# A two-layer decoder step on one core: layer 0's copies, its norm's bias and the opening's squares on other engines

## The chip, the cores and the metric

One core of one Trainium2 chip runs the whole program. The metric is the device time of one execution in microseconds. A core has five engines that matter here: TensorE (PE, matrix products, with a separate row PEld for its weight loads), VectorE (DVE), ScalarE (ACT), GpSimd (POOL), and SyncE (SP), whose queue issues all loads and stores of this kernel.

## The reference, cut to what matters

Two layers for 512 prompt positions and 32 sample positions (8 sequences of 4), model width 1024, all in fp32. Layer 0 norms its input, multiplies it by one wide matrix, and splits the columns into attention heads and convolution channels:

```
h = _rms(x, norm_g)
q, k, v, g_att, u_a, u_b, g_conv = _split(h @ w_in, AB_SPLITS)
q = _rms(q.reshape(B, T, ATT_HEADS, ATT_HEAD_DIM), q_g)
k = _rms(k.reshape(B, T, ATT_HEADS, ATT_HEAD_DIM), k_g)
u = u_a * jax.nn.sigmoid(u_b)
...
y = jax.nn.silu(_layernorm(y, ln_g, ln_b))
...
m = jnp.concatenate([o_att * jax.nn.silu(g_att), o_conv * jax.nn.silu(g_conv)], axis=-1)
return x + m @ w_out
```

`_rms` divides by the root of the mean square over the 1024 features and scales by `norm_g`. The prompt attends within blocks of 256 positions and to the earlier block; the samples attend to cached keys and values, which are gathered page by page. The convolution has 31 taps; its result goes through a layer norm with gain `ln_g` and bias `ln_b`. Layer 1 is a gated linear recurrence with its own projections; the change does not touch it.

## The kernel before, in words

**Layout.** Activations lie with features on the 128 partitions and the 544 positions along the row: `xT[k]`, k = 0..7, is 128 features by 544 positions. Every product is split in precision: a factor a is kept as a rounded high part and a low part a - high, and `unit` (L137) adds three passes for each k: high weight x high activation (L142), high weight x low activation (L143), low weight x high activation (L144). A unit makes 128 output features for one half (272) of the positions in one of three PSUM banks "g". `wtile` (L127) loads a weight tile from memory on SP's queue, makes its high part on ScalarE (L133) and its low part on VectorE (L134).

**Order.** The program is written with a tile framework (L1072) that plays it on its own model of the engines when it is built and chooses the order of each engine's instructions from that, on the queues of SP and GpSimd as well; at a few places an order is pinned by hand (`issue_after`). A changed engine for one instruction can therefore change the order of others.

**The opening** (L178 to L310) is written as steps "sA u nA u r sB w e a nB" (L292) on the two halves of the positions. `squares` (L256) makes the squares of the 8 feature tiles, two at a time (four instructions, the engine of each from `SQ` for the first half and `SQB` for the second: `sqg` on GpSimd at L186, `sqa` on ScalarE at L180, `sqv` on VectorE at L183), and for the first half also the gained inputs `xg` (L189 on ScalarE, L192 on VectorE). Three adds follow: squares 0 and 1 on GpSimd (L265), squares 2 and 3 on VectorE (L266), then both sums on VectorE (L267). `norms` (L249) sums over the partitions with PE (L252), takes the root on ScalarE (L253) and the reciprocal on VectorE (L254). Meanwhile two units "u" run in plain fp32 on `xg` (L230), `rawsplit` makes high (L272, ScalarE) and low (L273, VectorE) parts of the second half, `wsplits` the weight parts wh (L281) and wl (L282), and step "e" scales the two finished units by the norm (L235), which frees their PSUM banks. The third and fourth unit (L363, L142 to L144) need L273, L282, and a free bank.

**After the opening** three constants are cast to bf16 (`identb`, `causb`, `smb`, L312 to L317) for the masks of attention. For each of four pairs of heads `prepkq` (L388) projects and norms keys and queries: the keys are turned by PE, copied by ScalarE (L404), normed, stored, turned back, and copied out of PSUM (L447 on ScalarE; the sample columns `ksT` on VectorE, L448). `prepvg` (L451) projects the values, turns them, copies them out of PSUM (`vt` L462 and `vsn` L463, VectorE) and stores them. The turned tiles take two PSUM banks "t", which the attention's transposes share. `attend` (L478) does the attention of a pair; its exponentials are L496. The taps of the convolution (L379) run on VectorE all along.

**The layer norm** of the convolution (L555 to L595) ends, for each of 4 channel tiles and 2 halves, in a multiplication by gain and 1/deviation (L586, VectorE), the addition of the bias (L587, VectorE), a tanh (L589, ScalarE) and two products (L590, L591, VectorE). Beside it the cached key pages are loaded (L606) for the sample attention.

Of the kernel before, what the change touches and what calls it, by code (L numbers as in the profile page):

```python
# [13 lines left out]
AF = mybir.ActivationFunctionType  # L14
ALU = mybir.AluOpType
# [5 lines left out]
TS = 32  # L21
# [8 lines left out]
C_CAUS = 256  # L30
C_SM = 384
# [35 lines left out]
def hybrid_step(ctx, tc, xt_in, cache_kt, cache_v, conv_in, hgrn_in, page_table, par_in, k_norm_0,  # L67
# [3 lines left out]
    V, A, G, PE, SP = nc.vector, nc.scalar, nc.gpsimd, nc.tensor, nc.sync  # L71
# [17 lines left out]
    cst = cp.tile([128, C_END], F32, name="cst")  # L89
# [67 lines left out]
    def vec(name, k=0):  # L157
        return vecs[:, vidx[name] + k:vidx[name] + k + 1]
# [19 lines left out]
    with tc.tile_pool(name="l0", bufs=1) as lp:  # L178
# [13 lines left out]
            V.tensor_scalar(xg[k][:, hs], xT[k][:, hs], vec("n0", k), None, op0=ALU.mult)  # L192

        SQ = (sqg, sqa, sqa, sqv)
        SQB = (sqg, sqa, sqa, sqv)
        XG = (xga, xgv, xga, xgv, xga, xgv, xga, xgv, )
        NM = (V, V, V, V, V, V, V, V, )
        xg = [mtile(("xg", k), F32) for k in range(KT)]
# [57 lines left out]
        def squares(hf):  # L256
            sq = []
            for i in range(4):
                q = mk(lp, "kn", [128, T], 8).rearrange("p (a t) -> p a t", a=2)
                (SQ, SQB)[hf][i](q, xTall[:, 2 * i:2 * i + 2, HC[hf]])  # L260
                sq.append(q)
                if hf == 0:
                    for k in (2 * i, 2 * i + 1):
                        XG[k](k, HC[0])
            G.tensor_tensor(sq[0], sq[0], sq[1], op=ALU.add)  # L265
            V.tensor_tensor(sq[2], sq[2], sq[3], op=ALU.add)  # L266
            V.tensor_tensor(sq[0], sq[0], sq[2], op=ALU.add)  # L267
            return sq[0]
# [41 lines left out]
                norm_a()  # L310

        identb = lp.tile([128, 128], BF16, name="identb")  # L312
        G.tensor_copy(identb, ident)
        causb = lp.tile([128, 128], BF16, name="causb")
        G.tensor_copy(causb, cst[:, C_CAUS:C_CAUS + 128])
        smb = lp.tile([128, 64], BF16, name="smb")
        G.tensor_copy(smb, cst[:, C_SM:C_SM + 64])  # L317
        qbd = lp.tile([128, 4, NS, 32], F32, name="qbd")
        G.memset(qbd, 0.0)
        ksT = lp.tile([128, 4, TS], F32, name="ksT")  # L320
# [67 lines left out]
        def prepkq(c):  # L388
            col = c * 128
            kr = mk(lp, "kr", [128, T], 2)  # L390
            w = wtile(w_in_0, 512 + col)
            for hf in range(2):
                unit_to(kr, w, hf)
            kt = mk(lp, "kt", [128, 5, 128], 2)
            ksq = mk(lp, "P", [128, 512], 2).rearrange("p (i d) -> p i d", i=4)
            ksqs = mk(lp, "ksqs", [TS, 128], 1)
            ssk = mk(lp, "ssk", [128, 24], 2)
            pk = bank("t")
            pks = bank("t")
            for i, n, sl in TOK:  # L400
                transpose(pk[:, i * 128:(i + 1) * 128] if i < 4 else pks[:n, :128], kr[:, sl], 128)
            for pq, i0, i1, n, so in ((pk, 0, 4, 128, ksq), (pks, 4, 5, TS, ksqs.unsqueeze(1))):
                p3 = pq[:n, :(i1 - i0) * 128].rearrange("p (i d) -> p i d", d=128)
                A.activation(kt[:n, i0:i1], p3, AF.Copy)  # L404
                A.activation(so, p3, AF.Square)
            V.reduce_sum(ssk[:, 0:8], ksq.rearrange("p i (h d) -> p (i h) d", d=64), axis=AX.X)
            V.reduce_sum(ssk[:TS, 8:10], ksqs.rearrange("p (h d) -> p h d", d=64), axis=AX.X)

            w = wtile(w_in_0, col)
            qT = mk(lp, "qT", [128, T], 2)  # L410
            sq = mk(lp, "sq", [128, T], 1)
            for hf in range(2):
                unit_to(qT, w, hf)
                A.activation(sq[:, HC[hf]], qT[:, HC[hf]], AF.Square)
            pssq = bank("t")
            for i in range(4):
                PE.matmul(pssq[:, 2 * i:2 * i + 2], sq[:, i * 128:(i + 1) * 128], blk[:, 0:128:64], start=True, stop=True)
            PE.matmul(pssq[:, 8:8 + TS], blk, sq[:, TP:T], start=True, stop=True)
            rq = mk(lp, "rq", [128, 40], 2)
            rk = mk(lp, "rk", [128, 10], 2)  # L420
            A.activation(rq, pssq[:, 0:40], AF.Sqrt, bias=eps)
            A.activation(ssk[:, 0:8], ssk[:, 0:8], AF.Sqrt, scale=1.0 / 64, bias=eps)
            A.activation(ssk[:TS, 8:10], ssk[:TS, 8:10], AF.Sqrt, scale=1.0 / 64, bias=eps[:TS])
            V.reciprocal(rk[:, 0:8], ssk[:, 0:8])
            V.reciprocal(rk[:TS, 8:10], ssk[:TS, 8:10])
            V.reciprocal(rq, rq)
            for hh in range(2):
                r = slice(64 * hh, 64 * hh + 64)
                o = (2 * c + hh) * 4
                V.scalar_tensor_tensor(qbd[r, c, :, o:o + 4], qT[r, TP:T].rearrange("p (n t) -> p n t", t=4),  # L430
                                       gq8[r], rq[r, 8:40].rearrange("p (n t) -> p n t", t=4),
                                       op0=ALU.mult, op1=ALU.mult)
            kT = kz[c % 2]
            for i0, i1, n in ((0, 4, 128), (4, 5, TS)):
                k3 = kt[:n, i0:i1].rearrange("p i (h d) -> p (i h) d", d=64)
                nb = 2 * (i1 - i0)
                V.tensor_tensor(k3, k3, rk[:n, 2 * i0:2 * i1].unsqueeze(2).to_broadcast([n, nb, 64]), op=ALU.mult)
                V.tensor_tensor(k3, k3, gk_bc[:n].unsqueeze(1).to_broadcast([n, nb, 64]), op=ALU.mult)
            SP.dma_start(k_prompt[0].rearrange("(i p) h d -> p i (h d)", p=128)[:, :, col:col + 128], kt[:, 0:4])
            SP.dma_start(k_sample.rearrange("n t h d -> (n t) (h d)")[:, col:col + 128], kt[:TS, 4])  # L440
            pk = bank("t")
            pks = bank("t")
            for i, n, sl in TOK:
                transpose(pk[:, sl] if i < 4 else pks[:, :n], kt[:n, i], n)
            for hh in range(2):
                r = slice(64 * hh, 64 * hh + 64)
                A.activation(kT[r, hh], pk[r], AF.Copy, scale=gq8[r, 0:1])  # L447
            V.tensor_copy(ksT[:, c], pks[:, :TS])  # L448
            return c, rq, qT, kT

        def prepvg(c, rq, qT, kT):  # L451
            col = c * 128
            w = wtile(w_in_0, 1024 + col)
            vr = mk(lp, "kr", [128, T], 2)
            for hf in range(2):
                unit_to(vr, w, hf)
            vt = mk(lp, "vt", [128, 4, 128], 2)
            pk = bank("t")
            pks = bank("t")
            for i, n, sl in TOK:  # L460
                transpose(pk[:, i * 128:(i + 1) * 128] if i < 4 else pks[:n, :128], vr[:, sl], 128)
            V.tensor_copy(vt.rearrange("p i d -> p (i d)"), pk)  # L462
            V.tensor_copy(vsn[:, col:col + 128], pks[:TS, :128])  # L463
            SP.dma_start(v_prompt[0].rearrange("(i p) h d -> p i (h d)", p=128)[:, :, col:col + 128], vt)
            SP.dma_start(v_sample.rearrange("n t h d -> (n t) (h d)")[:, col:col + 128], vsn[:, col:col + 128])

            w = wtile(w_in_0, 1536 + col)
            ga = mk(lp, "ga", [128, T], 2)
            for hf in range(2):
                unit_to(ga, w, hf)  # L470
                tg = mk(lp, "tb", [128, HALF], 3)
                A.activation(tg, ga[:, HC[hf]], AF.Tanh, scale=0.5)
                V.scalar_tensor_tensor(ga[:, HC[hf]], tg, 1.0, ga[:, HC[hf]], op0=ALU.add, op1=ALU.mult)
            G.tensor_scalar(gas[:, c], ga[:, TP:T], 0.5, 0.0, op0=ALU.mult, op1=ALU.add)

            return c, rq, qT, kT, vt, ga
# [105 lines left out]
        for c in range(4):  # L582
            tgs = []
            for hf in range(2):
                hs = HC[hf]
                V.scalar_tensor_tensor(cy[c][:, hs], cy[c][:, hs], vec("lg", c), rss[hf], op0=ALU.mult, op1=ALU.mult)  # L586
                V.tensor_scalar(cy[c][:, hs], cy[c][:, hs], vec("lb", c), None, op0=ALU.add)  # L587
                tg = mk(lp, "ct", [128, HALF], 2)
                A.activation(tg, cy[c][:, hs], AF.Tanh, scale=0.5)  # L589
                V.scalar_tensor_tensor(tg, tg, 1.0, cy[c][:, hs], op0=ALU.add, op1=ALU.mult)  # L590
                V.scalar_tensor_tensor(tg, tg, 0.25, gc[c][:, hs], op0=ALU.mult, op1=ALU.mult)  # L591
                tgs.append(tg)
            mh, ml = mtile(("h", 4 + c)), mtile(("l", 4 + c))
            for hf in range(2):
                split(mh[:, HC[hf]], ml[:, HC[hf]], tgs[hf])  # L595
# [485 lines left out]
```

## Time and profile before

| | |
|---|---|
| median of 3 runs | 655.58 us (653.95 to 656.63) |
| the profiled execution | 655.62 us, of it span 652.9 us |
| PE busy in the span | 629.5 us, 5806 instructions |
| DVE busy | 524.8 us, 1252 instructions |
| ACT busy | 365.5 us, 908 instructions |
| POOL busy | 62.7 us, 91 instructions |

The profile is that of one execution. "Busy" is the time in which an engine has an instruction under way; matmuls are pipelined, so a busy PE need not be at its peak rate. The granted clock of TensorE (PEclk) is 1.00 at 2.4 GHz and 0.50 at 1.2 GHz. In a row of the timeline the bracket at the end gives the time for which the engine stood idle before the instruction, and the engine, tile and line that ended this wait.

### The profile page before, as it was taken

What the parts mean: (1) busy time and instruction counts of PE and PEld (TensorE: products, weight loads), DVE (VectorE), ACT (ScalarE), POOL (GpSimd) and SP (SyncE); (2) the same over time, 40 slices, a digit from 0 to 9 for tenths busy, and PEclk for the clock granted to TensorE, in tenths of its full rate; (3) what the DMA queues carried; (4) which work ended last, traced back from release to release, by engine and by line L of the source; (5) the groups of instructions that cost most, each with busy time, mean ns of one, the idle gap of its engine ahead of it and who ended that gap; (6) DMA issues with size and microseconds to landing.
All of it is one profiled execution on the core that took longest, in us unless ns stands there. A gap on an engine that the chain in (4) does not pass through costs nothing.

```text
span 652.9 us, 14858 instructions
## 1 busy us (share of the span) xinstructions
PE 629.5 (96%) x5806; PEld 581.9 (89%) x5806; DVE 524.8 (80%) x1252; ACT 365.5 (56%) x908; POOL 62.7 (10%) x91
## 2 busy tenths in 40 slices
PE   8799999999999986999989999999999999999997
PEld 6699998997996855879989999999999999999997
DVE  6999989889889857666978988878787878866656
ACT  7344486487378674445755664646464646447321
POOL 6100000000100000000011211111111110121000
PEclk9799999999999997999999999999999999999999
DMA  8434311221242047446442232323223232322114
GB/s 297 121 82 111 113 56 66 84 83 65 80 84 81 22 139 241 155 143 213 162 146 102 70 113 84 107 93 102 99 99 102 84 117 69 115 78 94 46 58 149
DMA packets 39015, 70.56 MB, mean 108 GB/s; under 512 B 11938, under 2 KB 20642, under 8 KB 38946
## 3 DMA queue, kind: packets, MB, share of 16 engines
q1 hardware_dynamic: 38946, 69.63, 33.6%
q8 instruction: 45, 0.74, 0.5%
q14 instruction: 24, 0.20, 0.1%
HBM read 59.88 MB, written 9.73 MB: 107 GB/s over the span
## 4 chain that ended last, share of the span: by engine, by line
PE 88%; DVE 4%; DMA 3%; ACT 3%; SPq 1%; issue 1%; DVEq 0%; ACTq 0%
PE g L142 23%; PE g L143 23%; PE g L144 22%; PE t L102 5%; PE s L484 2%; PE o L508 2%; DMA kn<-in_cache_kt_dram 2%; PE o L952 1%; PE t L939 1%; PE s L847 1%; DMA kn<-in_cache_v_dram 1%; PE s L612 1%; PE s L853 1%; DMA xTall<-in_xt_dram 1%; PE o L954 1%
## 5 line engine op out<-in xcount | busy, mean ns | idle before, releaser
L142 PE MATMUL g<-h,wh 128*128 128x272 f32 x944 | 278.9, 296 | 5.3 <-DVE ct L235 2.7
L143 PE MATMUL g<-h,wh 128*128 128x272 f32 x944 | 277.9, 295 | 1.9 <-DVE h L273 1.7
L144 PE MATMUL g<-h,wl 128*128 128x272 f32 x944 | 275.4, 292 | 0.0
L142 PEld LDWEIGHTS g<-h,wh 128*128 128x128 f32 x944 | 179.7, 190 | 9.7 <-ACT f L743 3.1
L143 PEld LDWEIGHTS g<-h,wh 128*128 128x128 f32 x944 | 179.6, 190 | 6.0 <-DVE h L273 3.1
L144 PEld LDWEIGHTS g<-h,wl 128*128 128x128 f32 x944 | 179.5, 190 | 1.7 <-issue 1.2
L133 ACT ACTIVATE wh<-wr 128x1024 fp32r<-128x1024 f32 (+4 forms) x90 | 88.1, 981 | 91.1 <-PE g L143 84.5
L134 DVE TENSOR_TENSOR wl<-wr,wh 128x1024 fp32r<-128x1024 f32 (+4 forms) x90 | 101.1, 1125 | 26.4 <-ACT wh L133 25.6
L379 DVE SCALAR_TENSOR_TENSOR m<-m,vecs,m 128x512 f32<-128x512 f32 x120 | 87.5, 741 | 0.7
L142 PE MATMUL g<-m,wh 128*128 128x272 f32 x256 | 74.0, 293 | 0.3 <-ACT wh L133 0.3
L144 PE MATMUL g<-m,wl 128*128 128x272 f32 x256 | 74.1, 291 | 0.0
L143 PE MATMUL g<-m,wh 128*128 128x272 f32 x240 | 69.6, 290 | 0.0
L142 PEld LDWEIGHTS g<-m,wh 128*128 128x128 f32 x256 | 47.9, 188 | 2.6 <-DVE m L106 0.8
L144 PEld LDWEIGHTS g<-m,wl 128*128 128x128 f32 x256 | 48.1, 189 | 1.0 <-issue 0.8
L143 PEld LDWEIGHTS g<-m,wh 128*128 128x128 f32 x240 | 45.2, 188 | 1.1 <-DVE ct L590 0.8
L959 ACT ACTIVATE S<-S,tot 128x128 f32<-128x128 f32 x64 | 20.5, 390 | 11.4 <-PE t L858 11.4
L484 PE MATMUL s<-kz,qT 128*128 128x128 f32 (+3 forms) x64 | 22.8, 447 | 1.4 <-ACT PP L496 1.3
L916 DVE TENSOR_TENSOR qq<-qq,tot 128x256 f32<-128x256 f32 x24 | 11.7, 486 | 14.8 <-PE s L888 12.0
L503 ACT ACTIVATE PT<-t 128x128 f32<-128x128 f32 (+3 forms) x32 | 13.9, 433 | 14.7 <-PE t L102 14.6
L961 POOL TENSOR_TENSOR ve<-vx,cst 128x1024 fp32r<-128x1024 f32 x8 | 16.1, 2019 | 49.8 <-DVE vx L736 30.0
L1020 DVE TENSOR_TENSOR xTall<-g,xTall 128x272 f32<-128x272 f32 x32 | 13.5, 437 | 8.8 <-PE g L144 8.3
L917 DVE TENSOR_TENSOR kk<-kk,tot 128x256 f32<-128x256 f32 (+1 forms) x48 | 20.0, 417 | 0.3
(300 smaller groups left out, 1018.6 us busy)
## 6 DMA issues: line engine op xcount, KB each, us to landing
wr<-in_w_in_dram SPq DMA_DIRECT2D x58, 512.0 KB, 3.6
wr<-in_w_out_dram SPq DMA_DIRECT2D x16, 512.0 KB, 3.7
kn<-in_cache_kt_dram SPq DMA_DIRECT2D x16, 256.0 KB, 3.6
kn<-in_cache_v_dram SPq DMA_DIRECT2D x16, 256.0 KB, 4.7
S<-in_hgrn_dram SPq DMA_DIRECT2D x8, 512.0 KB, 4.8
out_hgrns_dram<-S SPq DMA_DIRECT2D x8, 512.0 KB, 2.6
xTall<-in_xt_dram SPq DMA_DIRECT2D x8, 272.0 KB, 5.4
out_y_dram<-xTall SPq DMA_DIRECT2D x8, 272.0 KB, 2.1
```

The source lines that it names most:

```text
L102: PE.transpose(out, in_, ident[:np_, :np_])
L133: A.activation(wh, raw, AF.Copy)
L134: V.tensor_tensor(wl, raw, wh, op=ALU.subtract)
L142: PE.matmul(ps, wh[:, k - k0, :], ah, start=(k == k0), stop=False)
L143: PE.matmul(ps, wh[:, k - k0, :], al, start=False, stop=False)
L144: PE.matmul(ps, wl[:, k - k0, :], ah, start=False, stop=(k == k1 - 1))
L379: V.scalar_tensor_tensor(cy[c][:, :TP], up[c][:, j:j + TP], cw[:, c, j:j + 1], cy[c][:, :TP], op0=ALU.mult, op1=ALU.add)
L484: sc = PE.matmul(ss[hh][:, :L], qT[:, i * 128:(i + 1) * 128], kT[:, hh, 0:L], start=True, stop=False)
L503: A.activation(PT[:, :L], pT[:, :L], AF.Copy)
L917: V.tensor_tensor(k3[:, :, 0, :], k3[:, :, 0, :], t3[:, :, 1:2].to_broadcast([128, nblk, hsz]), op=ALU.mult)
L959: A.activation(S0[:, n], S0[:, n], AF.Copy, scale=tots[:, n:n + 1])
L961: G.tensor_tensor(ve, vx.unsqueeze(1).to_broadcast([128, NS, 128]), exm.unsqueeze(2).to_broadcast([128, NS, 128]), op=ALU.mult)
```

## The change

The adds of squares 0 and 1 go from GpSimd to VectorE, in both halves. The first square of the second half and three casts of constants go from GpSimd to ScalarE. The copies of the turned sample keys and of the turned values go from VectorE to ScalarE, and so does the addition of the layer norm's bias.

```diff
         SQ = (sqg, sqa, sqa, sqv)
-        SQB = (sqg, sqa, sqa, sqv)
+        SQB = (sqa, sqa, sqa, sqv)
...
-            G.tensor_tensor(sq[0], sq[0], sq[1], op=ALU.add)
+            V.tensor_tensor(sq[0], sq[0], sq[1], op=ALU.add)
             V.tensor_tensor(sq[2], sq[2], sq[3], op=ALU.add)
             V.tensor_tensor(sq[0], sq[0], sq[2], op=ALU.add)
...
-        G.tensor_copy(identb, ident)
+        A.activation(identb, ident, AF.Copy)
...
-        G.tensor_copy(causb, cst[:, C_CAUS:C_CAUS + 128])
+        A.activation(causb, cst[:, C_CAUS:C_CAUS + 128], AF.Copy)
...
-        G.tensor_copy(smb, cst[:, C_SM:C_SM + 64])
+        A.activation(smb, cst[:, C_SM:C_SM + 64], AF.Copy)
...
-            V.tensor_copy(ksT[:, c], pks[:, :TS])
+            A.activation(ksT[:, c], pks[:, :TS], AF.Copy)
...
-            V.tensor_copy(vt.rearrange("p i d -> p (i d)"), pk)
-            V.tensor_copy(vsn[:, col:col + 128], pks[:TS, :128])
+            A.activation(vt.rearrange("p i d -> p (i d)"), pk, AF.Copy)
+            A.activation(vsn[:, col:col + 128], pks[:TS, :128], AF.Copy)
...
-                V.tensor_scalar(cy[c][:, hs], cy[c][:, hs], vec("lb", c), None, op0=ALU.add)
+                A.activation(cy[c][:, hs], cy[c][:, hs], AF.Identity, bias=vec("lb", c))
```

## Rows read from the trace of the kernel before

**Rows 1.** The page's first part: busy us (share of the span) x instructions.

```profile
PE 629.5 (96%) x5806; PEld 581.9 (89%) x5806; DVE 524.8 (80%) x1252; ACT 365.5 (56%) x908; POOL 62.7 (10%) x91
```

**Rows 2.** Stretches: us, busy (instructions) of each engine, PEclk, DMA share, GB/s.

```profile
15.30:26.00 10.70, 6.08 (x31) 4.24 (x29) 10.70 (x16) 3.40 (x6) 3.06 (x6) 0.94 0.53 112
26.00:31.40 5.40, 5.40 (x24) 5.40 (x25) 4.92 (x12) 1.57 (x4) 0.00 (x0) 0.50 0.36 124
31.40:210.00 178.60, 178.48 (x1366) 164.16 (x1365) 160.51 (x311) 109.76 (x229) 5.85 (x8) 1.00 0.30 82
...
239.00:257.00 18.00, 10.67 (x168) 7.73 (x168) 11.76 (x29) 10.28 (x20) 0.00 (x0) 0.81 0.76 250
```

**Rows 3.** PE's waits, whole span: who waited for whom: total us, times, longest.

```profile
PE s L612 <- DMA kn<-in_cache_kt_dram: 6.0, 3, 3.0
PE g L142 <- DVE ct L235: 2.7, 1, 2.7
...
PE g L143 <- DVE h L273: 1.7, 3, 0.9
...
PE s L484 <- ACT PP L496: 1.3, 2, 0.6
```

**Rows 4.** Timeline of VectorE in the opening: start us, us, instruction.

```profile
6.27 0.36 DVE L192 TENSOR_SCALAR m<-xTall,vecs 128x272 f32<-128x272 f32 x1 [0.52 <-DMA xTall<-in_xt_dram]
7.52 1.27 DVE L192 TENSOR_SCALAR m<-xTall,vecs 128x272 f32<-128x272 f32 x1 [0.89 <-DMA xTall<-in_xt_dram]
...
12.21 2.11 DVE L282 TENSOR_TENSOR wl<-wr,wh 128x1024 fp32r<-128x1024 f32 x1
14.25 1.58 DVE L273 SCALAR_TENSOR_TENSOR h<-xTall,vecs,h 128x272 fp32r<-128x272 f32 x1
...
17.73 0.71 DVE L266 TENSOR_TENSOR kn<-kn,kn 128x544 f32<-128x544 f32 x1
18.37 0.49 DVE L273 SCALAR_TENSOR_TENSOR h<-xTall,vecs,h 128x272 fp32r<-128x272 f32 x1
...
22.66 1.21 DVE L134 TENSOR_TENSOR wl<-wr,wh 128x1024 fp32r<-128x1024 f32 x1
...
25.56 0.37 DVE L235 TENSOR_TENSOR ct<-g,kr 128x272 f32<-128x272 f32 x1
```

**Rows 5.** Timeline of GpSimd in the opening.

```profile
7.07 1.34 POOL L265 TENSOR_TENSOR kn<-kn,kn 128x544 f32<-128x544 f32 x1 [1.47 <-ACT kn L180]
...
11.07 2.17 POOL L186 TENSOR_TENSOR kn<-xTall 128x544 f32<-128x544 f32 x1 [2.43 <-DMA xTall<-in_xt_dram]
13.32 2.21 POOL L265 TENSOR_TENSOR kn<-kn,kn 128x544 f32<-128x544 f32 x1
15.48 0.50 POOL L313 CAST identb<-cst 128x128 bf16<-128x128 f32 x1
```

**Rows 6.** Timeline of ScalarE in the opening.

```profile
12.06 0.64 ACT L180 ACTIVATE kn<-xTall 128x544 f32<-128x544 f32 x1
12.61 0.51 ACT L272 ACTIVATE h<-xTall,vecs 128x272 fp32r<-128x272 f32 x1
...
21.58 0.49 ACT L253 ACTIVATE r1b<-t,eps 128x272 f32<-128x272 f32 x1 [3.91 <-PE t L252]
```

**Rows 7.** Copies by tile: ns min/median/max, first and last start us, shapes.

```profile
L404 ACT ACTIVATE kt<-t x8: 249/418/602, 53.8 to 186.0; 128x512 f32<-128x512 f32 x4, 32x128 f32<-32x128 f32 x4
...
L462 DVE COPY vt<-t x4: 680/687/692, 73.4 to 221.4; 128x512 f32<-128x512 f32 x4
```

**Rows 8.** The bias, by line: ns min/median/max, first and last start us.

```profile
L587 DVE TENSOR_SCALAR m<-m,vecs x8: 351/353/355, 250.6 to 262.3; 128x272 f32<-128x272 f32 x8
```

**Rows 9.** Timeline of ScalarE at 57 us: a table load and what follows.

```profile
57.30 1.28 ACT L422 ACT_TABLE_LOAD   x1
...
58.98 0.41 ACT L414 ACTIVATE sq<-qT 128x272 f32<-128x272 f32 x1
```

**Rows 10.** Waits, whole span: ScalarE for PE before the wide high part.

```profile
ACT wh L133 <- PE g L143: 84.5, 59, 4.5
```

## The prediction

> **What bounds the kernel now.** The page's first part comes first: TensorE (PE) is busy 96% of the span, VectorE (DVE) 80%, ScalarE (ACT) 56%, GpSimd (POOL) 10% [rows 1]. Work taken from an engine that is not the bound is worth something only where PE stands still, so the second view is the table by stretch [rows 2]. From 31.4 to 210 us PE is idle for 0.12 us of 178.6, with the full clock. It is idle in two places that the change touches: 15.3 to 26 us (6.08 of 10.7 us busy), followed by 5.4 us at half the clock, and 239 to 257 us (10.67 of 18). The list of PE's waits says for what [rows 3]: 6.0 us for pages of the key cache, 2.7 us for DVE's L235 in the opening, 1.7 us for DVE's low parts (L273), also in the opening, and 1.3 us for ScalarE's exponentials in attention. So the place to look at is DVE's order of work in the opening [rows 4], beside GpSimd's [rows 5] and ScalarE's [rows 6].
>
> In rows 4 the same instruction has two prices. L192 takes 0.36 us, and 1.27 when GpSimd's L265 runs beside it. The split wl takes 1.21 us, and 2.11 beside L186 of the second half. L273 takes 0.49, and 1.58 beside the second L265. Each two-operand instruction of GpSimd [rows 5] holds DVE up by 0.9 to 1.1 us, and is itself drawn out (2.2 us). DVE works without a gap worth naming from 7.5 us to L235 at 25.56, and PE resumes at 25.98: what DVE loses there, PE loses.
>
> **The change, part by part.**
>
> *Two adds L265, GpSimd to VectorE.* A DVE add of this size (L266) moves its successor by 18.37 - 17.73 = 0.64 us [rows 4]. First half: -0.91 (L192 1.27 to 0.36) + 0.64 = -0.27. Second half: -1.09 (L273 1.58 to 0.49) + 0.64 = -0.45.
>
> *Square L186 of the second half, GpSimd to ScalarE.* DVE gains 2.11 - 1.21 = 0.90 on wl. ScalarE gets one more L180, a step of 12.61 - 12.06 = 0.55 us [rows 6], ahead of the L272 that feed L273. DVE stands at wl and the first three L273 for longer than that, so I take 0; without that cover it is 0.55. The square of the first half stays on GpSimd, and so does its stretching of the first L192.
>
> *Three casts (identb, causb, smb), GpSimd to ScalarE.* GpSimd takes 0.50 us for one [rows 5]. On ScalarE I estimate 0.3 each from the small copy of L404 (0.25 us, rows 7), 0.9 together. ScalarE is idle 3.91 us before L253 at 21.58 [rows 6], and the first reader is the mask in attention, far later: 0. If they go ahead of the L272 instead, up to 0.9.
>
> Sum for DVE up to L235: -0.27 - 0.90 - 1.09 + 0.64 = **-1.62 us**, so L235 at about 23.94 and PE resumes at 24.36 in place of 25.98.
>
> *The clock.* From 26 to 31.4 us the granted clock is 0.50 and 24 of the long matmuls go through [rows 2]; at the mean of the next stretch (178.48 / 1366 = 0.131 us) they would need 3.1, so 2.3 are lost. The clock fell after PE had gone idle. Three cases: it rises at the same moment as now, and the 1.62 gained run at half speed (gain 0.8); it rises later by as much as PE resumes earlier (gain 1.62); it does not fall (gain 3.9). I take 1.62: PE's pause stays about as long, because L273 and L235 both move forward.
>
> *Copies of turned values and keys (L462, L463, L448), VectorE to ScalarE, four times.* The long one takes 0.69 us on DVE and 0.60 on ScalarE (L404, same shape); the two small ones are some 0.25 each there [rows 7]. ScalarE gets 4 x 1.1 = 4.4 us and DVE loses about as much. All but the last of the four lie in the stretch in which PE is never idle, so nothing can be gained there; what hides the cost is that PE works on other units while a bank is emptied. PE's waits for ScalarE's exponentials (1.3 us, rows 3) are the ceiling for a gain and show where a busier ScalarE would hurt: up to one 0.6 more per copy, 2.4 for four. I take 0.
>
> *The norm's bias (L587), eight times.* DVE loses 8 x 0.35 = 2.8 us [rows 8]. On ScalarE, with a per-partition operand and the same 272 columns, L272 takes 0.51 [rows 6], so 4.1 us. They lie between 250 and 263 us, where PE waits for cache pages and then works off the gate units: 0. Without that cover: 4.1 - 2.8 = 1.3 us slower. This function (Identity) does not occur in the trace. If it needs a table of its own, each switch is 1.28 us; but a Square runs 0.4 us after the table for the root was loaded, without a load of its own [rows 9], so simple functions do not switch. I take 0; the other end is four loads, 5.1 us of an engine that is half idle there. The Trainium skill, "ScalarE: Activation LUTs", section "Table sets: the hidden batching unit", lists identity among the functions in every set, which would make it 0; no row here shows Identity itself.
>
> The sum is 655.62 - 1.62 = 654.0 us against the profiled execution's own time (span 652.9, 2.7 us around it). The median of the runs, 655.58, is as good as the same.
>
> **The rivals.**
>
> *No gain.* ScalarE becomes the bound of the opening: 0.55 for the square and 0.9 for casts that the planner puts ahead of the L272 are 1.45 us, which eats the 1.62. Or the bias adds, dearer by 0.16 each, reach the path (+1.3). For: in the opening ScalarE feeds every L273. Against: its 3.91 us pause. Time 655.6; chance 0.18. The Trainium skill, "ScalarE: Activation LUTs", section "Rules for kernel authors", speaks for this one: adds and multiplications belong on VectorE. The rows agree for the bias (0.35 against 0.51), not for the long copy (0.69 against 0.60).
>
> *A larger gain.* The planner orders each engine by its own model, and the adds are now ready at other times. If L235 comes before PE has finished the third unit, PE has a free bank and doesn't pause: the 2.7 us of rows 3 and the 2.3 of the clock go, 655.6 - 5.0 = 650.6. That needs L235 about 2.6 us earlier, 1.0 more than the sum gives, so it decides whether wl (1.21 us, at 22.66) is moved behind L235. For: the norm's reciprocals have less in front of them. Against: an order is no part of the change. Chance 0.24.
>
> *Slower.* One mechanism: before L133 ScalarE stands idle until PE has freed a wide weight buffer, 84.5 us in 59 waits, 1.43 each, the longest 4.5 [rows 10], and whatever the planner has put behind L133 waits with it. A copy of turned values in that place keeps two banks occupied, and PE's next transposes stop. Price: 4 x 1.43 = 5.7 us, time 654.0 + 5.7 = 659.7. It decides from the point where PE has no unit left to run ahead of the transposes. Against: L404 empties the same banks from ScalarE today, and PE waits for it nowhere in rows 3. Chance 0.08.
>
> **How the numbers follow.** The forecast has 0.50. A measurement of this kernel can tell about 0.5%, 3.3 us, from no change: below 652.3 is faster, above 658.9 slower. Only the larger gain lies below (0.24), only the copies behind L133 above (0.08); forecast and no gain make 0.68 the same. The range runs from the larger gain, 650.6, to no gain with a run at the upper end of those shown, 656.6; the slower case is left out, with the far tail of the larger gain.
>
> **What would show it.** Right: wl and the L273 of the opening at 1.2 and 0.5 us throughout, GpSimd with a single two-operand instruction, L235 near 24 us, PE resuming 1.6 us earlier, and the stretch after that a copy of today's, shifted. PE's total idle time falls by about 1.6 us, and the matmuls between 32 and 210 us take the same time. Wrong: L235 still at 25.5; the granted clock not falling at all (the larger gain); new waits of PE's transposes for ScalarE's copies (slower); table loads beside L587; or a different wait before the cache pages at 239 us, which would mean that the planner, not the moved work, made the difference.

## The result, and the profile after

The changed kernel takes 646.0 us (median, 645.06 to 646.67); the kernel before, timed beside it, takes 654.8. The ratio is 0.987 (95% interval 0.9855 to 0.989): 1.3% faster. The forecast was 654.0 with a range down to 650.6, so the gain of 8.8 us is more than five times the 1.62 that was forecast, and the time lies below the range. The profiled execution took 645.54 us, its span 643.6.

The page's first part after, against [rows 1]:

```profile
PE 625.1 (97%) x5806; PEld 579.2 (90%) x5806; DVE 517.3 (80%) x1234; ACT 374.7 (58%) x932; POOL 55.9 (9%) x85
```

The work has moved as the diff says: DVE 7.5 us less, ACT 9.2 more, POOL 6.8 less. PE is busy for 4.4 us less with the same 5806 instructions, at a mean granted clock of 0.992 in place of 0.987: most of the 4.4 us are matmuls that no longer run at half the clock. PE also stands still for 4.9 us less. The stretches, against [rows 2] (us, busy (instructions) of PE, PEld, DVE, ACT, POOL, then PEclk, DMA share, GB/s):

```profile
15.30:26.00 10.70, 8.04 (x56) 7.31 (x55) 10.70 (x17) 5.74 (x12) 1.95 (x2) 1.00 0.54 106
26.00:31.40 5.40, 5.40 (x46) 5.40 (x45) 5.40 (x12) 2.19 (x4) 0.00 (x0) 1.00 0.40 121
...
235.00:253.00 18.00, 13.95 (x179) 11.51 (x179) 12.10 (x23) 11.30 (x19) 0.00 (x0) 0.72 0.70 224
```

In the opening PE gets 56 matmuls done where it did 31, and behind it 46 where it did 24, with the clock never falling. The waits of PE, whole span, against [rows 3]:

```profile
PE s L612 <- DMA kn<-in_cache_kt_dram: 4.1, 2, 2.1
...
PE t L252 <- DVE kn L267: 1.7, 1, 1.7
...
PE g L142 <- DVE ct L235: 1.0, 1, 1.0
```

The wait for L235 is 1.0 in place of 2.7, and the 1.7 for L273 became 1.7 for L267 (the sum of squares of the second half). The 6.0 us for key pages in three waits became 4.1 in two. PE's row behind the wait for L235, first before, then after:

```profile
25.98 0.59 PE L142 MATMUL g<-h,wh 128*128 128x272 f32 x1 [2.68 <-DVE ct L235]
```

```profile
22.68 0.39 PE L142 MATMUL g<-h,wh 128*128 128x272 f32 x1 [0.97 <-DVE ct L235]
```

VectorE's opening, against [rows 4]:

```profile
10.57 2.35 DVE L282 TENSOR_TENSOR wl<-wr,wh 128x1024 fp32r<-128x1024 f32 x2
12.84 0.91 DVE L273 SCALAR_TENSOR_TENSOR h<-xTall,vecs,h 128x272 fp32r<-128x272 f32 x2
...
16.81 1.84 DVE L254 RECIPROCAL kr<-kr 128x272 f32<-128x272 f32 x1
18.58 0.66 DVE L267 TENSOR_TENSOR kn<-kn,kn 128x544 f32<-128x544 f32 x1
19.16 1.98 DVE L273 SCALAR_TENSOR_TENSOR h<-xTall,vecs,h 128x272 fp32r<-128x272 f32 x3
21.06 1.21 DVE L134 TENSOR_TENSOR wl<-wr,wh 128x1024 fp32r<-128x1024 f32 x1
22.19 0.43 DVE L235 TENSOR_TENSOR ct<-g,kr 128x272 f32<-128x272 f32 x1
...
23.95 1.84 DVE L254 RECIPROCAL r1b<-r1b 128x272 f32<-128x272 f32 x1
```

The two wl take 2.35 us together, where one alone took 2.11, and six of the eight L273 take 0.49. That is what was forecast. The other two L273 take 0.82 each (they are in the row of three above), while GpSimd runs its L335, which multiplies one tensor; before, one L273 did. But there is a second thing: the **order** is another one. Before, the reciprocal of the first half (kr) stood behind L273 of k = 6, and that of the second half (r1b, 1.84 us) stood ahead of L235. Now kr is ahead of the last three L273, and r1b is behind both L235. So L235 comes 25.56 - 22.19 = 3.4 us earlier: 1.84 of it is a reciprocal that stepped aside, and 1.5 is left for the forecast's sum of 1.62.

The bias and the long copy on ScalarE (ns min/median/max), against [rows 7, 8]:

```profile
L587 ACT ACTIVATE m<-m,vecs x8: 506/509/522, 241.6 to 254.6; 128x272 f32<-128x272 f32 x8
...
L462 ACT ACTIVATE vt<-t x4: 593/598/600, 69.7 to 214.1; 128x512 f32<-128x512 f32 x4
```

SP's queue changed as well, though the diff touches no load. Its issues at the key pages, first before, then after (start, us from first to last issue):

```profile
227.52 11.21 SPq L130 DMA_DIRECT2D wr<-in_w_out_dram  x2
239.00 17.16 SPq L606 DMA_DIRECT2D kn<-in_cache_kt_dram  x16
```

```profile
220.84 0.35 SPq L130 DMA_DIRECT2D wr<-in_w_out_dram  x1
221.45 3.03 SPq L606 DMA_DIRECT2D kn<-in_cache_kt_dram  x6
233.40 0.34 SPq L130 DMA_DIRECT2D wr<-in_w_out_dram  x1
236.53 11.39 SPq L606 DMA_DIRECT2D kn<-in_cache_kt_dram  x10
```

Before, the first key page stood in the queue behind a weight tile that waited 11 us for a buffer. Now six pages go ahead of that tile.

### The profile page after: what moved, and what is told of

The parts are those of the page before. It is cut to its first block, busy times and chain, and to the rows that moved or that the text cites. A ratio compares the mean times of both kernels' runs of the same rounds, so it can differ in the third digit from the quotient of the medians.

```text
span 643.6 us, 14850 instructions
## 1 busy us (share of the span) xinstructions
PE 625.1 (97%) x5806; PEld 579.2 (90%) x5806; DVE 517.3 (80%) x1234; ACT 374.7 (58%) x932; POOL 55.9 (9%) x85
## 4 chain that ended last, share of the span: by engine, by line
PE 87%; DVE 6%; ACT 3%; DMA 2%; issue 1%; SPq 1%; DVEq 0%; ACTq 0%
PE g L142 23%; PE g L143 22%; PE g L144 22%; PE t L102 5%; PE s L484 2%; PE o L508 2%; PE o L952 1%; PE t L939 1%; PE s L847 1%; DMA kn<-in_cache_kt_dram 1%; DVE wl L134 1%; PE s L612 1%; DMA wr<-in_w_in_dram 1%; PE s L853 1%; PE o L954 1%
```

## The experiments

The theories. **Order**: the planner, fed with other engines, wrote another order of VectorE in the opening and of SP and PE at the key pages, and that is most of the gain. **Contention**: it is GpSimd's two-operand work, gone from beside VectorE's. Further rivals are named where they are tried. Beside the medians, each kernel's trace is compared with that of the kernel before, matmul by matmul: how many us earlier the n-th of the 5806 matmuls starts.

```
kernel         median   n=200  n=1600  n=2200  n=2600  n=5700
                       (opening)      (keys) (boundary)
changed         646.0    +5.3    +7.1    +7.6    +9.1    +9.3
a4_casts        653.3    +3.3    +3.5    +0.2    +1.7    +1.7
a1_opening      649.3    +6.1    +7.0    +6.6    +6.8    +6.9
a2_copies       654.8    +0.1    +1.2    -0.4    +1.1    +1.3
a3_bias         655.2    +1.0    +1.0    -0.4    -0.5    -0.3
b1_neworder     653.0    +4.6    +4.8    +2.9    +2.9    +3.0
c2_nobias       649.2    +5.4    +7.1    +4.3    +4.2    +4.4
c1_nocopies     645.4    +5.1    +5.6    +7.5    +9.0    +9.1
b3_keys         653.4    +0.3    +0.3    +2.0    +1.9    +1.9
b2_oldorder     651.8    +2.8    +3.2    +2.4    +3.8    +4.0
e1_biasorder    646.2    +5.7    +7.5    +7.2    +8.7    +8.9
d1_units        649.4    +5.5    +7.2    +7.3    +7.3    +7.5
d2_units_wl     647.7    +6.0    +7.7    +6.7    +6.8    +6.9
f1_orderonly    649.2    +3.7    +3.9    +5.2    +6.7    +6.9
o2_c1_wl        645.8    +5.3    +5.8    +8.8   +10.2   +10.4
d4              653.9    +5.7    +7.4    +2.4    +1.1    +1.3
```

The medians of the kernel before beside them were 654.3 to 654.9. A row is one execution: a3_bias has the old order of PE and SP and still differs from before by 1.0 in the opening and by 1.4 at the keys, so a single difference under 1.5 us there says little. The medians decide between kernels; the table says where.

**The three casts alone** (SQB, L265, copies and bias as before).

```diff
-        G.tensor_copy(identb, ident)
+        A.activation(identb, ident, AF.Copy)
...
-        G.tensor_copy(causb, cst[:, C_CAUS:C_CAUS + 128])
+        A.activation(causb, cst[:, C_CAUS:C_CAUS + 128], AF.Copy)
...
-        G.tensor_copy(smb, cst[:, C_SM:C_SM + 64])
+        A.activation(smb, cst[:, C_SM:C_SM + 64], AF.Copy)
```

> Only the three casts go to ScalarE; GpSimd keeps its squares and adds. The built order of VectorE in the opening is nevertheless the new one: the first half's reciprocal ahead of the last low parts L273, and L235 ahead of the second half's reciprocal. Theory 'order' (the gain in the opening comes from L235 being earlier in VectorE's queue, so that PE finds a bank free and its clock doesn't fall): most of the opening's 5.3 us is here already, 3.5 to 5.3 us by the 100th matmul, no granted clock of 0.5 after 26 us. Theory 'contention' (VectorE is no longer stretched by GpSimd's two-operand instructions): at most 1 us by the 100th matmul, since L186 and both L265 still run on GpSimd and stretch L192, wl and L273 by about 1 us each, and the clock falls as before.

Measured: 653.3 us, ratio 0.998 (0.997 to 0.999); +3.2 by the 100th matmul, and no half clock in the opening. GpSimd's squares and adds were all still there. That is a little under the 3.5 that 'order' expected and far over the 1 of 'contention': most of the opening's gain comes with an edit that takes nothing off VectorE. L235 comes at 24.22, only 1.3 us earlier than before, but PE waits 0.97 us for it in place of 2.68. The gain was given back at the key pages.

**The opening's squares and adds alone.**

```diff
-        SQB = (sqg, sqa, sqa, sqv)
+        SQB = (sqa, sqa, sqa, sqv)
...
-            G.tensor_tensor(sq[0], sq[0], sq[1], op=ALU.add)
+            V.tensor_tensor(sq[0], sq[0], sq[1], op=ALU.add)
```

> The opening's squares and adds alone (L265 on VectorE, the first square of the second half on ScalarE); casts stay on GpSimd, copies and bias as before. Its order in the opening is the new one too. Both theories expect the opening's 5 us here (4.5 to 5.5 by the 100th matmul); 'order' expects not over 1.5 us more than the kernel with the casts alone, 'contention' 3 us or more beyond it. Whether the 1.5 us at the layer boundary and the 1 to 2 us at the key pages come too tells whether they belong to the opening's edits: the queue of loads has the same new order as the changed kernel, so I expect 6 to 9 us in all; 5 if those belong to the copies or the bias.

Measured: 649.3 us, 0.994 (0.992 to 0.996); +6.0 by the 100th matmul. That is 2.8 beyond the casts alone, between what the two theories said (up to 1.5, and 3 or more), so both have a part. The 6 to 9 us in all were too much: 5.0.

**The copies alone, and the bias alone.**

```diff
-            V.tensor_copy(ksT[:, c], pks[:, :TS])
+            A.activation(ksT[:, c], pks[:, :TS], AF.Copy)
...
-            V.tensor_copy(vt.rearrange("p i d -> p (i d)"), pk)
-            V.tensor_copy(vsn[:, col:col + 128], pks[:TS, :128])
+            A.activation(vt.rearrange("p i d -> p (i d)"), pk, AF.Copy)
+            A.activation(vsn[:, col:col + 128], pks[:TS, :128], AF.Copy)
```

> The copies of turned values and sample keys alone on ScalarE. The opening is as before, so 0 by the 100th matmul under both theories. My own theory: 0 from the copies themselves between 50 and 220 us, within 0.5 us; six key pages ahead of a weight tile in SP's queue, as in the changed kernel, worth 0.5 to 1.5 us at the key pages; in all 0.5 to 1.5 us faster. Rival: the copies leave VectorE or the exponentials earlier and bring the 1.1 us that the changed kernel gains between 100 and 125 us; then 1.5 to 2.5 us faster.

```diff
-                V.tensor_scalar(cy[c][:, hs], cy[c][:, hs], vec("lb", c), None, op0=ALU.add)
+                A.activation(cy[c][:, hs], cy[c][:, hs], AF.Identity, bias=vec("lb", c))
```

> The bias adds L587 alone on ScalarE; the orders of PE and SP are those of the kernel before. Theory: 0 (within 0.5 us) and no table load beside the eight Identity instructions, 0.44 us each. Rival: they free VectorE before the layer boundary and bring the 1.5 us there that the changed kernel gains: 1 to 2 us faster. Second rival: ScalarE is late for the tanh behind them, up to 1.3 us slower.

Measured: copies 654.8 us, ratio 1.000 (0.998 to 1.002); bias 655.2, 1.001 (0.999 to 1.003). Neither is worth anything alone; for the copies 0.5 to 1.5 us had been expected, for six early key pages. By the medians (654.3 before) the four parts alone gain 1.0, 5.0, -0.5 and -0.9: 4.6 of 8.8 us. The parts don't add up, which moved work alone would not lead one to expect.

**Order alone in the opening:** the kernel before, every engine as it was, two pins on VectorE.

```diff
+                with (tc.issue_after(recs[0].ins) if k >= 5 else nullcontext()):
                     last = V.scalar_tensor_tensor(hh_[KT + k][:, HC[1]], xT[k][:, HC[1]], vec("n0", k), hh_[k][:, HC[1]],
...
+            with (tc.issue_after(scl[1].ins) if hf else nullcontext()):
                 recs.append(V.reciprocal(rbc[hf], rbc[hf]))
```

> The kernel before, every instruction on its old engine; only VectorE's order in the opening is pinned to the new one (the low parts L273 of k = 5 to 7 behind the first half's reciprocal, the second half's reciprocal behind both L235). 'Order': 3 us by the 100th matmul, as with the casts alone (3.2), and no half clock at 26 us; 'contention': 0, within 0.5. The end depends on the key pages: PE's queue has, as with the casts alone, the third and fourth group of key products straight behind each other, so I expect the gain to be given back there and 653 to 654 us in all.

Measured: 653.0 us, 0.9985 (0.997 to 0.9998); +4.5 by the 100th matmul, where 3 was expected and 'contention' said 0. Between 25 and 30 us, the same columns as the stretches above:

```profile
25.00:30.00 5.00, 5.00 (x42) 5.00 (x41) 5.00 (x8) 1.28 (x2) 0.00 (x0) 1.00 0.28 107
```

42 matmuls, as in the changed kernel (17 in the kernel before, at a clock of 0.50). GpSimd still holds VectorE up, and L235 comes 2.6 us earlier all the same (the lines are numbered for this kernel; L286 is L282):

```profile
10.55 3.25 DVE L286 TENSOR_TENSOR wl<-wr,wh 128x1024 fp32r<-128x1024 f32 x2
22.92 0.42 DVE L235 TENSOR_TENSOR ct<-g,kr 128x272 f32<-128x272 f32 x1
```

**The old order with the changed kernel's engines.** This is the case that the forecast described.

```diff
-            V.reciprocal(rbc[hf], rbc[hf])
+            if hf:
+                recs.append(V.reciprocal(rbc[hf], rbc[hf]))
...
+                if k == 6:
+                    with tc.issue_after(last.ins):
+                        V.reciprocal(rbc[0], rbc[0])
...
-                us0 = [scaled(us0[u], 0, u) for u in range(2)]
+                with tc.issue_after(recs[0].ins):
+                    us0 = [scaled(us0[u], 0, u) for u in range(2)]
...
-        for step in "sA u nA u r sB w e a nB".split():
+        for step in "sA u nA u r sB w nB e a".split():
```

> The changed kernel, all its engines, but VectorE's order in the opening pinned to the old one: the first half's reciprocal behind the low part L273 of k = 6, both L235 behind the second half's reciprocal. This is the case that the forecast of 654.0 described. 'Order': L235 at about 24 us (22.2 in the changed kernel plus a reciprocal of 1.84), PE waits over 2 us for it, the granted clock falls to 0.50 afterwards, and by the 100th matmul 1 to 2.5 us are gained of the 5.2. 'Contention': 4 us or more. The key pages are ordered as in the changed kernel, so behind the opening the same 2 to 3.5 us come as there: 648 to 650.5 in all by 'order', 646.5 or less by 'contention'.

Measured: 651.8 us, 0.994 (0.992 to 0.997), slower than was expected by either theory. In the opening it went as 'order' said. VectorE:

```profile
20.81 1.21 DVE L134 TENSOR_TENSOR wl<-wr,wh 128x1024 fp32r<-128x1024 f32 x1
21.95 1.84 DVE L257 RECIPROCAL r1b<-r1b 128x272 f32<-128x272 f32 x1
23.71 0.37 DVE L235 TENSOR_TENSOR ct<-g,kr 128x272 f32<-128x272 f32 x1
```

and PE's wait:

```profile
24.14 0.55 PE L142 MATMUL g<-h,wh 128*128 128x272 f32 x1 [2.68 <-DVE ct L235]
```

L235 at 23.71 and PE resuming at 24.14: the forecast had said 23.94 and 24.36. The pause is as long as before (2.68), the clock falls behind it, and by the 200th matmul 2.8 us are gained. So the forecast's sum for VectorE was right for the order it assumed.

**The changed kernel without the copies, and without the bias** (each the reverse of the diff above).

> The changed kernel with the copies of turned values and keys back on VectorE. PE's order at the key pages is that of the changed kernel (97 matmuls between the third and the fourth group). 'PE's order at the key pages': within 1 us of the changed kernel, 646 to 647; the copies are worth at most the 0.7 to 1 us that the attention gains between 100 and 215 us. Rival 'copies': 2.5 us or more slower, 648.5 to 649.5, as with the opening's edits alone.

> The changed kernel with the bias adds back on VectorE. With them back, PE's built order has the fourth group of key products straight behind the third; in the changed kernel 97 matmuls of the gate units stand between. Theory 'PE's order at the key pages' (the bias move is worth something only through this order): three waits for key pages in place of two, 1.5 to 3 us slower than the changed kernel, 647.5 to 649; nothing differs before 235 us by more than 0.5. Rival 'copies': what the changed kernel has beyond the opening's edits comes from the copies, so that this kernel stays within 0.7 us of it.

Measured: without the copies 645.4 us, 0.986 (0.985 to 0.988), as fast as the changed kernel. Without the bias 649.2, 0.9915 (0.989 to 0.994): 3.2 us slower. Both as the theory of PE's order at the key pages said. Of PE's four groups of key products, 32 matmuls each, those after the first, in the changed kernel:

```profile
241.04 1.91 PE L612 MATMUL s<-kn,qbd 128*32 128x128 f32 x32 [2.06 <-DMA kn<-in_cache_kt_dram]
245.67 1.93 PE L612 MATMUL s<-kn,qbd 128*32 128x128 f32 x32 [2.00 <-DMA kn<-in_cache_kt_dram]
262.28 1.08 PE L612 MATMUL s<-kn,qbd 128*32 128x128 f32 x32
```

and in the one without the bias:

```profile
241.71 1.08 PE L612 MATMUL s<-kn,qbd 128*32 128x128 f32 x32 [1.15 <-DMA kn<-in_cache_kt_dram]
245.72 1.87 PE L612 MATMUL s<-kn,qbd 128*32 128x128 f32 x32 [2.42 <-DMA kn<-in_cache_kt_dram]
250.28 1.94 PE L612 MATMUL s<-kn,qbd 128*32 128x128 f32 x32 [2.68 <-DMA kn<-in_cache_kt_dram]
```

With the bias on VectorE the planner puts the fourth group straight behind the third, where its pages are not there yet; with the bias on ScalarE the 96 matmuls of four gate units stand between, and it waits for nothing.

**The bias back on VectorE, with that order pinned.**

```diff
-                A.activation(cy[c][:, hs], cy[c][:, hs], AF.Identity, bias=vec("lb", c))
+                V.tensor_scalar(cy[c][:, hs], cy[c][:, hs], vec("lb", c), None, op0=ALU.add)
...
-                pin = None
+                at = {(1, 1): 7}.get((g, j))
+                pin = None if at is None else gm[at]
```

(gm holds the last matmul of each gate unit; 7 is the last one.)

> The changed kernel with the bias adds back on VectorE (which by itself was 649.2 us) and one pin: the fourth group of key products behind the last gate unit, which is the changed kernel's order of PE. If the bias move is worth something only through this order: 645.5 to 647, two waits for key pages, all of the 3.2 us back. If VectorE's 2.8 us less work counts by itself: 648 us or more.

Measured: 646.2 us, 0.988 (0.985 to 0.9905). 3.0 of the 3.2 us are back: by these medians it was the order, and the engine of the bias is worth nothing that can be told.

**The order of the loads alone**, in the kernel before.

```diff
+                with (tc.issue_after(kld[5].ins) if c == 3 and not hf else nullcontext()):
+                    w = wtile(w_out_0, c * 128)
-                ps = unit(wtile(w_out_0, c * 128), m, hf)
+                ps = unit(w, m, hf)
```

> The kernel before with one edit: the load of the last w_out tile of this stage stands behind the sixth key page in SP's queue, as in the changed kernel. If the early key pages are worth something by themselves: one of PE's three waits for key pages gone, 1 to 2 us faster by the 2100th matmul, 652.5 to 653.5. If not (the pages only move the wait to the next group): within 0.5 us. The opening as before.

Measured: 653.4 us, 0.998 (0.996 to 0.999): 1.4 us, two waits for key pages (5.1 us together) in place of three.

**Both orders alone:** every instruction on its old engine, the opening's two pins and the pin of the fourth key group.

> The kernel before with every instruction on its old engine and two pins of order alone: VectorE's opening order of the changed kernel, and the fourth group of key products behind the last gate unit. 'Order' (the changed kernel is faster through the planner's new order, at the opening and at the key pages, not through the moved work): 4.5 us by the 100th matmul as with the opening's pin alone, 1 to 2 us more at the key pages, 646.5 to 648.5 in all, 3 us or more faster than the opening's pin alone (653.0). 'Engines' (the moved work counts): the second pin brings nothing, 651 or more.

Measured: 649.2 us, 0.991 (0.990 to 0.993). 3.8 below the opening's pins alone, so the second pin counts, against 'engines'; but not 646.5 to 648.5. Six key pages go ahead of the weight tile here too, without a pin, as they do in the kernel with the opening's pins alone; so all three orders are in it. Order alone makes 5.7 of the 8.8 us.

**Trying to fill the last waits for key pages.** In the first, key groups two to four are pinned behind gate units; the second also pins the wl that stands ahead of L235 (1.21 us at 21.06 in the changed kernel) behind both L235; in the third the gates of channel tiles 2 and 3 are also written ahead of the layer norm's sums; the fourth is the kernel without copies with only the pin of wl.

```diff
+                at = {(0, 1): 4, (1, 0): 5, (1, 1): 7}.get((g, j))
...
-        with tc.issue_after(split_.ins):
+        with tc.issue_after(scl[1].ins):
```

> The changed kernel with PE's order at the key pages pinned further: the second group of key products behind the first gate unit of channel tile 2, the third behind its second, the fourth behind the last of tile 3. The built order puts all 97 gate matmuls ahead of the second group and 36 of the output product ahead of the fourth. If the waits for key pages are time lost (4.1 us, and half the clock for 10 us around them): 2 to 6 us faster than the changed kernel, 640 to 644. Rival: the pages' own transfer bounds the stage, and the waits move to the value pages: within 1 us of it, 645 to 647.

> As the one with the gate units between the key groups, and in the opening the low part wl of the fourth weight tile (1.2 us) pinned behind both L235 on VectorE. L235 comes 1.1 us earlier, so the 0.97 us that PE still waits for it goes: 0.5 to 1 us faster than without. If PE then waits for something else in its place (the wide low part itself, or L273): within 0.3.

> The changed kernel with the last two channel tiles' gates written ahead of the layer norm's sums, and the key groups pinned behind gate units, so that the sums' products (which the earlier such kernel put ahead of the gates, where PE stood 5.4 us for VectorE) come later. If the waits for key pages (4.1 us) are time that gate units can fill: waits for keys and for the sums under 2 us together, 641 to 645. Rival: the pages' transfers bound the stage, and the wait moves to the value pages or the sums: 646 or more.

> The changed kernel without the copies (645.4 us by itself), and with wl of the fourth weight tile pinned behind both L235 on VectorE. If PE's 0.8 us wait for L235 is what that low part costs: 0.5 to 1 us earlier by the 100th matmul (the pair with gate units showed 0.8), 644.4 to 645.2 in all. Rival: the key pages take it back, 645.4 or more.

Measured: 649.4, 647.7, 653.9 and 645.8 us; ratios 0.992 (0.990 to 0.995), 0.988 (0.986 to 0.991), 0.999 (0.997 to 1.000) and 0.986 (0.983 to 0.988). None of the four came to the time that was hoped for. The waits for keys went in the first, but a product of the layer norm's sums came ahead of the gate units and stood for VectorE instead:

```profile
PE g L578 <- DVE kn L575: 5.4, 1, 5.4
```

The third waits 6.0 us for key pages, 2.0 for the sums and 1.9 for a copy of the samples' transposed weights. The pin of wl took the first wait for L235 away, for 0.5 us in the opening with the gate units and 0.2 without (n = 200). In the kernel without them the granted clock fell nevertheless (0.65 from 20 to 24 us), behind a wait of 1.9 us for L267; in the kernel without the copies a wait of 2.0 us for L267 was not followed by that. No kernel is faster than the changed one by more than the intervals.

## Why the prediction was wrong

**What was right.** That only places where PE stands still count; that VectorE's order in the opening decides; the prices 0.9 to 1.1 us for each stretched instruction. (That GpSimd's own are drawn out to 2.2 us holds for the two of the second half; the first half's L265 takes 1.34 [rows 5].) The sum of 1.62 is there: the old order with the new engines brings L235 to 23.71 us (forecast 23.94), 1.85 earlier than before, and in the new order the new engines bring about as much: at n = 200 the three kernels with GpSimd's old squares and adds (a4, b1, f1) gain 3.9 on average, the changed one 5.3, the others with the new engines 5.1 to 6.1. Three casts on ScalarE, 0.24 to 0.29 each (forecast 0.3), cost nothing, though they went between the L272, where the forecast had put up to 0.9: VectorE's rows have no gap there.

**The step that failed: the rival "A larger gain", at "Against: an order is no part of the change".** The sum kept today's order on every engine and moved only durations, and so had L273 and L235 move together and PE's pause stay as long. The runs showed that either of two small edits (the casts alone; the squares and adds alone) leads to the new order, and that the order is the larger part: 3.2 to 4.5 us by the 100th matmul with nothing taken off VectorE. The rival looked for it at wl, 1.21 us at 22.66; wl stayed ahead of L235, and a reciprocal of 1.84 us moved behind. The condition "about 2.6 us earlier" was met, with 3.4, and yet 1.0 us of the pause stayed, for the third unit too ended 1.6 us earlier (21.7 in place of 23.3). It was not the right measure either. With the casts alone L235 came only 1.3 us earlier, PE waited 0.97, and the clock stayed at 1.00; in the old order with the new engines it came 1.85 earlier, PE waited 2.68, and the clock fell. What the order changes is how long L235 comes behind the end of PE's third unit.

**The clock.** Of the three cases the forecast took the middle one. In its own scenario (old order) L235 moved 1.85 and 2.8 were gained, with a granted clock of 0.79 from 24 to 32 us in place of 0.57. But the clock there is 0.79 as well with the copies, the bias or the loads alone, whose openings are not edited, and those gain 0.5 on average (n = 200). So the middle case fits, and the further 1 us is not shown to be the edit's. In the new order the clock didn't fall, the third case.

**What had no price at all: the key pages.** The prediction named "a different wait before the cache pages" as a sign that the planner made the difference, and gave it 0 us. In SP's queue and in PE's, edits that have nothing to do with pages decide how many waits there are. Early pages alone are worth 1.4 us. From n = 1600 to 2200 the five kernels with early pages whose fourth group follows the third at once (a4, a1, a2, b1, c2) lose 2.0 us on average against before (0.5 to 3.3); the seven where gate units stand between (changed, c1, b3, b2, e1, f1, o2) gain 1.0 on average (from a loss of 0.9 to a gain of 3.0).

**The copies: 0, right.** Before the pages the changed kernel is 1.4 us ahead of the one without them (n = 1600), and behind the pages they are level: both wait for the same transfers. **The bias: 0, right for the engine, wrong for the kernel.** It takes 0.51 us on ScalarE, as taken from L272, and 25 table loads are there before and after, so Identity brought none. (The Trainium skill, "ScalarE: Activation LUTs", section "Table sets: the hidden batching unit", has it in every set; the trace agrees.) Its order brought about 3 us. (The Trainium skill, "ScalarE: Activation LUTs", section "Rules for kernel authors", by which adds belong on VectorE, would have kept it there; the longer instruction, 0.51 against 0.35, is real and cost nothing.)

**What stays open.** 1.5 us of the traces' difference stand at the boundary to layer 1 (n = 2600). There PE pauses 2.65 us in every kernel, and behind it the clock fell before and not after. First the kernel before, then the changed one, from PE's first matmul on:

```profile
342.20:346.00 3.80, 3.73 (x18) 3.74 (x19) 3.16 (x9) 1.80 (x4) 0.00 (x0) 0.56 0.85 337
```

```profile
334.60:338.40 3.80, 3.77 (x30) 3.77 (x31) 3.24 (x10) 2.36 (x4) 0.00 (x0) 1.00 0.91 329
```

Of the 17 kernels profiled it didn't fall in 8, among them the copies alone and not the bias alone; no edit explains that. Executions of one and the same kernel differ in this too: of 29 of the kernel before, timed beside the casts, 11 have a mean granted clock of 0.987 and a span of 652.3 us on average, and 5 have 0.989 and 651.1. So the 1.5 us may belong to the execution and not to the kernel; one trace of each can't tell. Order alone leaves 3.2 us to the changed kernel, of which the opening's shorter work is 1.6 in the traces (n = 200); the rest was not traced to one place. The old opening order on the new engines costs 5.8 us by the medians, more than an opening should: the traces put 2.5 in the opening (n = 200), 1.3 in attention (to n = 1600), 1.4 at the keys, and 1.8 behind the last matmul, which ends 5.5 us before the span does in that trace and 3.8 in the changed kernel's. Why the later three come with that order is not shown; four other traces (a1, a2, d2, o2) have such a long end too.

## What to carry to other kernels

Where a planner orders each engine by its own model, a moved instruction is also a new order, on queues that the diff doesn't name; before pricing durations, ask which order stands a hair from flipping, and what PE would gain or lose by it. An edit that gains through order can be had by a pin: a reciprocal that nobody waits for doesn't belong ahead of the multiplication that frees a PSUM bank, a page load not behind a weight load that waits for a buffer, and a product whose data come late not ahead of units that could run. Measure the parts alone and left out: alone they made 4.6 of 8.8 us, and one that is worth 0 alone was worth 3.2 in company.

## What was not expected of the hardware

That an instruction of VectorE can make almost no headway while one of GpSimd's works. In the changed kernel GpSimd's square L186 runs from 4.50 to 5.59 us, and L192 of VectorE, begun at 4.47, ends at 5.99: 0.40 us behind it, where L192 takes 0.36 alone.

```profile
4.50 1.09 POOL L186 TENSOR_TENSOR kn<-xTall 128x544 f32<-128x544 f32 x1 [0.37 <-DMA xTall<-in_xt_dram]
```

```profile
4.47 1.52 DVE L192 TENSOR_SCALAR m<-xTall,vecs 128x272 f32<-128x272 f32 x1 [3.59 <-DMA xTall<-in_xt_dram]
```

Before, the same L192 took 1.29 and ended 0.16 us behind the same L186, so the loss is 0.9 to 1.2 us beside 1.09 of GpSimd's work: about as long as that, not exactly. [rows 4, 5] can be read so as well: L186 (11.07 to 13.24) begins while VectorE is at its first wl and takes 2.17 in place of 1.09, and the second wl, begun at 12.21, ends 1.1 us behind L186 and takes 2.11 in place of 1.21. That each stands for the other in turn is argued from these times, not shown. (The Trainium skill, "SBUF — State Buffer", section "SBUF: two separate sides", calls the pair of ports that they share an exclusive lock for which the one that starts second stands still. The rows agree on the standing still, not on who: L192 began 0.03 us earlier and waited.)
